# A two-layer hybrid block on one core: a block of matrix products ahead of the first projection, the first norm's factors in an earlier transfer, a new order of work in the mixers, and one gate half in another arithmetic

## The chip, the core and the metric

The kernel runs on 1 core of one Trainium2 chip. The metric is the device time of one execution in microseconds. Before the change the median of 3 runs is 876.97 us (876.23 to 877.3). The engines of the core work from queues of their own, each in the order in which its instructions were issued: the tensor engine (PE: weight loads and matrix products), the vector engine (DVE), the scalar engine (ACT), GpSimd (POOL), and SyncE (SP), which only issues transfers.

## The reference, cut to what matters

Two layers, 256 positions, width 1024. Each layer is a mixer and a feed-forward part, each behind an RMS norm.

```
def s5_mixer(u, ...):                       # u: 512 wide, 32 groups of 16
    bu = einsum('bsgh,gph->bsgp', uf, b)    # 64 complex states a group
    x = associative_scan(complex_affine_combine, (a, f * bu), axis=1)
    y = re(einsum('bsgp,ghp->bsgh', x, c)) + d * uf
    z_val, z_gate = split(gelu(y) @ w_glu, 2)
    return z_val * sigmoid(z_gate)

def hybrid_mixer(h, ...):
    u, q, k_cmp, v_cmp, k_sel, v_sel, k_win, v_win, nsa_gate, g_ssm, g_nsa = split(h @ w_in, ...)
    y_ssm = s5_mixer(u, ...) @ w_branch_ssm
    y_nsa = nsa_mixer(rope(q), rope(k_cmp), ...) @ w_branch_nsa   # 3 kinds of attention, 8 heads
    return (sigmoid(g_ssm) * y_ssm + sigmoid(g_nsa) * y_nsa) @ w_out

def conv_ffn(h, ...):
    a, b = split(h @ w_in, 2)               # 2 x 2816
    return (gelu(causal_conv3(a) + conv_b) * b) @ w_out

for l in range(2):
    x = x + hybrid_mixer(rmsnorm(x, norm_mix[l]), ...)
    x = x + conv_ffn(rmsnorm(x, norm_ffn[l]), ...)
return rmsnorm(x, norm_final)
```

## The kernel before, in words

Activations lie transposed: 128 features on the partitions, 8 blocks of features, 256 positions as the moving side of a product. Weights stream from HBM in blocks of 128x1024 (512 KB) through a ring of 5 buffers (`raw`, L142). SP issues these transfers in program order. The norm's per-feature factors (`g_mix`) are multiplied in before the products (`xg`, L424), its per-position factor afterwards, when a result is read from PSUM (`rb`, L403).

There are two arithmetics for a product of 128 features by 256 positions. In the first layer's mixer it is full precision (L413, L437): one product, which the trace holds as two records. Elsewhere (L164 to L166) both sides are split into a rounded high part and a remainder, and three products are summed: `wh*ah`, `wh*al`, `wl*ah`. There ACT makes the high part of each weight block (`wh`, L153), and DVE the remainder (`wl`, L155).

A mixer is written as a list of short items, `ORDER` (L55), one string for each layer. `A:q:h` are the input products of state-space group q (half h) and DVE's turn into rotated coordinates (`psb`, `bc`, `bs`, `z`), `B` and `C` the scans over the two position halves, `D` the products of states and rotation (`pr`) and the output products (`psy`). `kc`, `ks`, `q`, `v` are projections, `cw`, `ck`, `cv` the compressed keys and values, `ac`, `at` the attention over them, `as` the scores and softmax of the other two kinds, `av` their transposes and value products (`ps_t`, `pT`, `ps_o`). `g:m:i` is half i of gate m, 8 gates in all: 8 blocks of weights by 256 positions into one half of a PSUM bank (`ps_g`), and after the second half one multiplication on DVE and one tanh on ACT (`th`, L811, L814). The items are issued in this order; a scheduler then places each instruction on its engine by priority, and products marked `row()` stay together. The gates take turns with other projections in two PSUM banks (tag `mm`), all else has six (`aux`). Behind the items come the GLU (`ps_glu`), the branch products (`ps_br`) and the output projection.

At the start (L123 to L139, L941 to L945) SP issues the two halves of x and the first two weight blocks in turn, ACT the transfers of `ssp` (the state-space parameters) and `sp` (all other small parameters). ACT makes squares for the norm (L360, L363) and `xg`, and PE begins with `psu` (U, L437).

Of the kernel before, what the change touches and what calls it, by code (L numbers as in the profile page):

```python
# [4 lines left out]
F32 = mybir.dt.float32  # L5
F32R = mybir.dt.float32r
BF = mybir.dt.bfloat16
I32 = mybir.dt.int32
AF = mybir.ActivationFunctionType
# [4 lines left out]
L = 2  # L14
T = 256
KD = 8
NF = 22
NS = 16
# [21 lines left out]
for _name, _w in [("ropec", 256), ("ropes", 256), ("ident", 128), ("causal", 128),  # L40
# [8 lines left out]
ENG = dict(t0="VV", c0="V", t1="VV", c1="V", cy="G", nacc="V", ma="V", sw="VG", z="VV", pr="VVVVVVVV")  # L49

NRAW, NWH, NWL, NSS, NSW, NRT, NPT, NZ, NTH = 5, 3, 3, 4, 1, 2, 2, 2, 8
HP = (400, 0)
AHEAD = (3, 4, 5, 6)

ORDER = [o.split() for o in (  # L55
# [10 lines left out]


def chunk_plan():
# [19 lines left out]
def body(tc, ctx, d, out):  # L88
    from contextlib import ExitStack
    nc = tc.nc  # L90
    V, S, G, PE = nc.vector, nc.scalar, nc.gpsimd, nc.tensor
    pool = lambda name, bufs=1, **k: ctx.enter_context(tc.tile_pool(name=name, bufs=bufs, **k))
    cst = pool("cst")
    raws = pool("raws", NRAW)

    pad = lambda name, n: pool(name).tile([128, n // 4], F32, name=name)
    pad("pad0", 128)
    whs = pool("whs", NWH)
    pad("pad3", 128)
    wls = pool("wls", NWL)  # L100
# [1 line left out]
    pp = pool("pp")  # L102
# [3 lines left out]
    psm = pool("psm", 1, space=PSUM)  # L106
# [6 lines left out]
        o += n  # L113


    ssp = cst.tile([128, 3 * L * NS + 14], F32, name="ssp")
    cc = cst.tile([128, NCC], F32, name="cc")

    def cslice(name):
# [3 lines left out]
    x = pp.tile([128, KD, T], F32, name="x", tag="x")  # L123
    dram = pool("dram", 1, space=bass.MemoryType.DRAM)
    xd = dram.tile([128, KD, T], F32, name="xd")
    spt = [cst.tile([128, NSP], F32, name=f"sp{l}") for l in range(L)]
    S.dma_start(ssp, d["ssp"])
    S.dma_start(spt[0], d["sp"][0])
    nc.sync.dma_start(x[:, 0:4, :], d["xT"][:, 0:4, :])

    def sp(l, name):
        a, w = _cols[name]
        return spt[l][:, a:a + w]

    ones = cst.tile([128, 128], F32, name="ones")
    V.memset(ones, 1.0)
    zero2 = cst.tile([128, 2], F32, name="zero2")
    V.memset(zero2, 0.0)
    S.activation(zero2, zero2, AF.Square)  # L139


    def raw(l, nm):  # L142
        o, n = where[nm]
        t = raws.tile([128, CH], F32, name="raw", tag="raw")
        src = bass.AP(tensor=d["wst"].tensor, offset=128 * (l * per_layer + o), ap=[[n, 128], [1, n]])
        nc.sync.dma_start(t[:, :n], src)
        return t, n

    def split(l, nm):

        t, n = raw(l, nm)
        h = whs.tile([128, CH], F32R, name="wh", tag="wh")
        S.copy(h[:, :n], t[:, :n])  # L153
        lo = wls.tile([128, CH], F32R, name="wl", tag="wl")
        V.tensor_tensor(lo[:, :n], t[:, :n], h.bitcast(F32)[:, :n], op=OP.subtract)  # L155
        return h, lo
# [37 lines left out]
    par = cst.tile([128, 5, N2], F32, name="par")  # L194
# [154 lines left out]
    class Norm:  # L349
        def __init__(self, l, gname, x, split=True):  # L350
            self.x = x
            self.g = sp(l, gname)
            if split:
                self.ah = pp.tile([128, KD, T], F32R, name="ah", tag="ah")
                self.al = pp.tile([128, KD, T], F32R, name="al", tag="al")
            self.acc = wk.tile([128, T], F32, name="nacc", bufs=1)
# [47 lines left out]


    def mixer(l, nm, sc, first, mp, sm_):
        if l:
            ah, al = nm.ah, nm.al

        def proj(ps, w):  # L410
            if not isinstance(w, tuple):
                for k in range(KD):
                    PE.matmul(ps, w[:, k * 128:(k + 1) * 128], xg[:, k, :], start=k == 0, stop=k == KD - 1,  # L413
                              skip_group_check=True)
                return
            for k in range(KD):
                wh, wl = wt(w, k)
                mm3(ps, wh, wl, ah[:, k, :], al[:, k, :], k == 0, k == KD - 1)


        if l == 0:
            xg = mp.tile([128, KD, T], F32, name="xg", bufs=1)
            for k in range(KD):
                S.activation(xg[:, k, :], nm.x[:, k, :], AF.Copy, scale=nm.g[:, k:k + 1])  # L424
            for k in range(KD):
                nm.square(k)
# [3 lines left out]
        for h in range(2):  # L430
# [3 lines left out]
            for k in range(KD):  # L434
                for i in range(2):
                    if l == 0:
                        PE.matmul(psu[i][:, :T], cu[i][0][:, k * 128:(k + 1) * 128], xg[:, k, :], start=k == 0,  # L437
                                  stop=k == KD - 1, skip_group_check=True)
# [257 lines left out]
        at = {}  # L696
# [101 lines left out]

        th = {}

        def gates(m, h=None):

            if h != 1:
                th[m] = bank("ps_g")
            ps = th[m]
            for i in (0, 1) if h is None else (h,):
                n = f"g{8 * i + m}"
                proj(ps[:, i * T:(i + 1) * T], raw(l, n)[0] if l == 0 else split(l, n))
            if h == 0:
                return  # L810
            t = lt.tile([128, 2, T], F32, name="th", tag="th", bufs=NTH)  # L811
            tt(t, ps.rearrange("p (a t) -> p a t", a=2), rb[:, None, :].to_broadcast([128, 2, T]), OP.mult)
            S.activation(t, t, AF.Tanh, scale=0.5)
            th[m] = t  # L814

        def gates_held(m, h=None):

            with tc.issue_after(at["hold"].ins):
# [1 line left out]

        parts = {"kc": p_kc, "ks": p_ks, "q": p_q, "v": p_v, "cin": c_in, "cw": c_w1, "ck": c_k, "cv": c_v, "par": p_par,
                 "pf": p_pf, "tb": p_tb, "mb": p_mb, "mc": p_mc, "ac": a_cmp, "at": a_cmpt, "as": a_s, "av": a_v,
                 "g": gates, "gh": gates_held, "A": ssm_a, "B": ssm_b2, "C": ssm_c2, "D": ssm_d}
        for item in ORDER[l]:
            f, *a = item.split(":")
            parts[f](*map(int, a))
# [113 lines left out]

    nm = Norm(0, "g_mix", x, False)  # L941
    first = [raw(0, "u0")]
    nc.sync.dma_start(x[:, 4:8, :], d["xT"][:, 4:8, :])
    first += [raw(0, "u1"), None, None]
    nc.sync.dma_start(cc, d["cc"])  # L945
    identb = cst.tile([128, 128], BF, name="identb")
    V.tensor_copy(identb, cslice("ident"))
# [125 lines left out]
    return s  # L1073


def ssm_small(p):

    fact = [1.0]
    for i in range(1, 16):
        fact.append(fact[-1] * i)  # L1080
    sin = [1.0 / fact[13], -1.0 / fact[11], 1.0 / fact[9], -1.0 / fact[7], 1.0 / fact[5], -1.0 / fact[3], 1.0]
    cos = [-1.0 / fact[14], 1.0 / fact[12], -1.0 / fact[10], 1.0 / fact[8], -1.0 / fact[6], 1.0 / fact[4], -1.0 / fact[2]]
    c = np.array([sin, cos], np.float32).T.reshape(1, 14)
    return np.concatenate([np.concatenate(p, axis=2).reshape(128, -1), np.repeat(c, 128, axis=0)], axis=1)


def const_array():
# [50 lines left out]
```

## Time and profile before

| | |
|---|---|
| runs shown, median of 3 | 876.97 us |
| profiled execution | 873.18 us |
| its span, first to last instruction | 871.1 us |
| mean granted clock of the tensor engine | 0.963 |
| busy: PE, DVE, ACT | 93%, 79%, 48% |

The first mixer takes the time up to about 200 us, its output projection and the feed-forward part go to about 430, the second mixer to about 633, the rest to the end. In a row of the timeline the number before "us" is the start, the next the length, "x" the count of instructions merged, and the bracket the idle time ahead with what ended it. A product's record ends only when its result has drained, so records that follow each other overlap, and the pace is read from many of them.

### The profile page before, as it was taken

To read this page: it belongs to the slowest core of one execution; us is meant where nothing else is said; L and a number is where in the kernel's file an instruction comes from. 1 tells how busy PE (TensorE), PEld (TensorE's weight loads), DVE (VectorE), ACT (ScalarE), POOL (GpSimd) and SP (SyncE) were. 2 spreads that over 40 slices of the span, in tenths; PEclk is the share of its full clock that TensorE was granted. 3 is DMA by queue.
4 is the path that set the end of the run, shared out by engine and by line. 5 is a ranking of instruction groups with operands and counts; after the bars stand their busy time and mean duration, and the time that the engine had idled before them with its cause. 6 is when DMAs were issued, how large, how long until landed. Compare 5 with 4: busy or idle time off the path is not lost.

```text
span 871.1 us, 16396 instructions
## 1 busy us (share of the span) xinstructions
PE 808.7 (93%) x6456; PEld 733.6 (84%) x6456; DVE 689.6 (79%) x1325; ACT 421.6 (48%) x783; POOL 25.4 (3%) x58
## 2 busy tenths in 40 slices
PE   5998999899989999999998889986899999999994
PEld 5886787469989999999998579763699999999994
DVE  6999766957998988877857998858588888888553
ACT  3211136575544665556522247755546555555440
POOL 0001000000000000000001030100000000000000
PEclk9999999799999999999999899967999999999997
DMA  6647635205645666658744663411155565655631
GB/s 245 192 115 254 216 106 168 77 25 159 183 148 166 192 195 194 194 183 271 242 143 117 236 201 133 134 60 49 64 175 183 184 194 194 194 194 194 193 124 49
DMA packets 41773, 142.42 MB, mean 163 GB/s; under 512 B 5216, under 2 KB 6752, under 8 KB 41696
## 3 DMA queue, kind: packets, MB, share of 16 engines
q1 hardware_dynamic: 39712, 139.15, 50.2%
q10 hardware_dynamic: 1984, 2.23, 0.9%
q8 instruction: 50, 0.82, 0.4%
q14 instruction: 27, 0.22, 0.1%
HBM read 136.38 MB, written 2.10 MB: 159 GB/s over the span
## 4 chain that ended last, share of the span: by engine, by line
PE 76%; DVE 14%; DMA 3%; ACT 3%; issue 3%; POOL 0%; ACTq 0%; DVEq 0%; SPq 0%
PE ps_f L165 9%; PE ps_f L166 9%; PE ps_f L164 9%; PE ps_g L413 5%; PE ps_fo L166 5%; PE ps_fo L165 5%; PE ps_fo L164 5%; DVE z L575 3%; PE psu L437 2%; PE ps_g L165 2%; PE ps_br L164 2%; PE ps_g L166 2%; PE ps_br L165 2%; PE ps_br L166 2%; PE ps_g L164 2%
## 5 line engine op out<-in xcount | busy, mean ns | idle before, releaser
L153 ACT CAST wh<-raw 128x1024 fp32r<-128x1024 f32 (+1 forms) x199 | 207.4, 1046 | 219.8 <-PE ps_f L165 99.0
L155 DVE TENSOR_TENSOR wl<-raw,wh 128x1024 fp32r<-128x1024 f32 (+1 forms) x199 | 242.6, 1221 | 66.7 <-ACT wh L153 66.1
L165 PE MATMUL ps_f<-al,wh 128*128 128x256 f32 x704 | 195.4, 278 | 2.4 <-DVE al L208 2.4
L164 PE MATMUL ps_f<-ah,wh 128*128 128x256 f32 x704 | 195.4, 278 | 1.8 <-DVE x L208 1.2
L166 PE MATMUL ps_f<-ah,wl 128*128 128x256 f32 x704 | 195.2, 277 | 0.8 <-DVE wl L155 0.8
L165 PEld LDWEIGHTS ps_f<-al,wh 128*128 128x128 f32 x704 | 132.9, 189 | 2.6 <-DVE al L208 2.6
L164 PEld LDWEIGHTS ps_f<-ah,wh 128*128 128x128 f32 x704 | 132.9, 189 | 2.1 <-ACT wh L153 2.1
L166 PEld LDWEIGHTS ps_f<-ah,wl 128*128 128x128 f32 x704 | 133.0, 189 | 1.0 <-DVE wl L155 1.0
L165 PE MATMUL ps_fo<-fl,wh 128*128 128x256 f32 x352 | 97.0, 276 | 0.0
L164 PE MATMUL ps_fo<-fh,wh 128*128 128x256 f32 x352 | 96.9, 276 | 0.0
L166 PE MATMUL ps_fo<-fh,wl 128*128 128x256 f32 x352 | 96.8, 276 | 0.0
L164 PEld LDWEIGHTS ps_fo<-fh,wh 128*128 128x128 f32 x352 | 66.1, 188 | 0.0
L165 PEld LDWEIGHTS ps_fo<-fl,wh 128*128 128x128 f32 x352 | 66.1, 188 | 0.0
L166 PEld LDWEIGHTS ps_fo<-fh,wl 128*128 128x128 f32 x352 | 65.9, 188 | 0.1
L413 PE MATMUL ps_g<-xg,raw 128*128 128x256 f32 x256 | 59.8, 389 | 0.0
L413 PEld LDWEIGHTS ps_g<-xg,raw 128*128 128x128 f32 x256 | 48.6, 194 | 8.0 <-issue 1.2
L199 DVE TENSOR_TENSOR pr<-z,E 128x512 f32<-128x512 f32 x64 | 41.7, 700 | 6.8 <-PE psy L610 6.7
L208 DVE SCALAR_TENSOR_TENSOR cv<-ab,sp,cv 128x255 f32<-128x255 f32 (+1 forms) x88 | 41.8, 480 | 1.4
L575 DVE TENSOR_TENSOR_SCAN z<-rm,z 128x512 f32<-128x512 f32 x32 | 38.8, 1244 | 1.5 <-POOL z L199 1.5
L166 PE MATMUL ps_g<-ah,wl 128*128 128x256 f32 x128 | 37.2, 290 | 0.6 <-DVE wl L155 0.5
L165 PE MATMUL ps_g<-al,wh 128*128 128x256 f32 x128 | 37.2, 291 | 0.0
L164 PE MATMUL ps_g<-ah,wh 128*128 128x256 f32 x128 | 36.8, 288 | 0.0
(260 smaller groups left out, 1705.7 us busy)
## 6 DMA issues: line engine op xcount, KB each, us to landing
raw<-wst SPq DMA_DIRECT2D x248, 512.0 KB, 4.3
x<-xT SPq DMA_DIRECT2D x4, 512.0 KB, 5.0
raw<-wst SPq DMA_DIRECT2D x4, 420.0 KB, 3.8
xd<-x SPq DMA_DIRECT2D x2, 512.0 KB, 7.3
x<-xd SPq DMA_DIRECT2D x2, 512.0 KB, 4.4
sw<-rt SPq DMA_DIRECT2D x12, 64.0 KB, 3.1
sw<-rt ACTq DMA_DIRECT2D x12, 64.0 KB, 4.2
raw<-wst SPq DMA_DIRECT2D x2, 280.0 KB, 2.8
```

What stands on the lines that cost most here:

```text
L153: S.copy(h[:, :n], t[:, :n])
L155: V.tensor_tensor(lo[:, :n], t[:, :n], h.bitcast(F32)[:, :n], op=OP.subtract)
L164: PE.matmul(ps, wh, ah, start=start, stop=False, **k)
L165: PE.matmul(ps, wh, al, start=False, stop=False, **k)
L166: PE.matmul(ps, wl, ah, start=False, stop=stop, **k)
L199: return e.tensor_tensor(o, a, b, op=op)
L208: e.scalar_tensor_tensor(o, a, s, b, op0=op0, op1=op1)
L413: PE.matmul(ps, w[:, k * 128:(k + 1) * 128], xg[:, k, :], start=k == 0, stop=k == KD - 1, skip_group_check=True)
L437: PE.matmul(psu[i][:, :T], cu[i][0][:, k * 128:(k + 1) * 128], xg[:, k, :], start=k == 0, stop=k == KD - 1, skip_group_check=True)
L575: V.tensor_tensor_scan(f, rt.rearrange("p a t -> p (a t)"), f, 0.0, op0=OP.mult, op1=OP.add)
```

## The change

There are five edits. Ahead of U, PE multiplies a 128x128 block of ones by itself 14 times, into a PSUM tile that nothing reads. The first norm's 8 factor columns are appended to `ssp`, and `xg` takes them from there. The second half of x is issued after the second weight block instead of before it. An item `sa` in the first mixer splits `xg` into high part and remainder, and an item `gs` makes a gate half in the arithmetic of the three products; it is used for `g:1:1` alone. Both strings of `ORDER` are new.

```
 NRAW, NWH, NWL, NSS, NSW, NRT, NPT, NZ, NTH = 5, 3, 3, 4, 1, 2, 2, 2, 8
+WARM = 14
 ORDER = [
-    ('par tb:0 pf q:1 q:0 mb kc cin tb:1 A:0:0 A:0:1 ks B:0 v A:1:0 A:1:1 g:0:0 g:0:1 g:1:0 g:1:1 cw:0:0 cw:0:1 '
+    ('par tb:0 q:1 kc mb q:0 pf cin tb:1 A:0:0 A:0:1 B:0 ks v A:1:0 A:1:1 sa g:0:0 g:0:1 g:1:0 cw:0:0 cw:0:1 '
...
-     'as:1:1:1:1 B:3 av:1:0 D:2:0 D:2:1 g:5:0 g:5:1 g:7:0 g:7:1 g:0:0 g:0:1 C:3 g:3:0 g:3:1 g:6:0 g:6:1 av:1:1 '
+     'as:1:1:1:1 D:2:0 g:5:0 g:5:1 g:7:0 g:7:1 g:0:0 g:0:1 D:2:1 g:3:0 g:3:1 C:3 g:2:1 g:6:0 g:6:1 av:1:1 D:3:0 '
...
-    pad("pad0", 128)
+    pad("pad0", 96)
...
-    ssp = cst.tile([128, 3 * L * NS + 14], F32, name="ssp")
+    ssp = cst.tile([128, 3 * L * NS + 22], F32, name="ssp")
...
+    nc.sync.dma_start(x[:, 0:4, :], d["xT"][:, 0:4, :])
     S.dma_start(ssp, d["ssp"])
     S.dma_start(spt[0], d["sp"][0])
-    nc.sync.dma_start(x[:, 0:4, :], d["xT"][:, 0:4, :])
...
+    warm = psm.tile([128, 512], F32, name="warm", tag="aux", bufs=6)
+    for i in range(WARM):
+        PE.matmul(warm[:, :128], ones, ones, start=i == 0, stop=i == WARM - 1, skip_group_check=True)
...
-            self.g = sp(l, gname)
+            self.g = ssp[:, 3 * L * NS + 14:] if l == 0 and gname == "g_mix" else sp(l, gname)
...
-        def gates(m, h=None):
+        def p_sa():
+
+            nonlocal ah, al, xg
...
+            ah = pp.tile([128, KD, T], F32R, name="ah", tag="ah")
+            al = pp.tile([128, KD, T], F32R, name="al", tag="al")
+            for k in range(0, KD, 4):
+                split_act(ah[:, k:k + 4, :], al[:, k:k + 4, :], xg[:, k:k + 4, :])
+
+        def gates_other(m, h=None):
+            gates(m, h, l == 0)
+
+        def gates(m, h=None, sp=l > 0):
...
-                proj(ps[:, i * T:(i + 1) * T], raw(l, n)[0] if l == 0 else split(l, n))
+                proj(ps[:, i * T:(i + 1) * T], split(l, n) if sp else raw(l, n)[0])
...
     first = [raw(0, "u0")]
+    first += [raw(0, "u1"), None, None]
     nc.sync.dma_start(x[:, 4:8, :], d["xT"][:, 4:8, :])
-    first += [raw(0, "u1"), None, None]
```

On PE the program now starts with the ones, and a projection of q stands between the two halves of U. Before:

```order
L437 MATMUL psu<-xg,raw 128x256 x16
L382 MATMUL ps_n<-ones,nacc 128x1 x2
L382 MATMUL ps_n<-ones,sq 128x1 x2
L437 MATMUL psu<-xg,raw 128x256 x16
L413 MATMUL ps_q_405<-xg,raw 128x256 x10
```

and now:

```order
L144 MATMUL warm<-ones 128x128 x14
L442 MATMUL psu<-xg,raw 128x256 x16
L417 MATMUL ps_q_404<-xg,raw 128x256 x8
L387 MATMUL ps_n<-ones,nacc 128x1 x2
L442 MATMUL psu<-xg,raw 128x256
L387 MATMUL ps_n<-ones,sq 128x1 x2
```

The sums of the norm (`ps_n`) move behind that half of q.

On ACT at the start the block xg is now made in two parts, with the casts of `sa` (`ah`) between the squares. Before:

```order
L360 ACTIVATE nacc<-x 128x256
L363 ACTIVATE sq<-x 128x256 x3
L424 ACTIVATE xg<-x,sp_101 128x256 x8
L363 ACTIVATE sq<-x 128x256 x4
L159 CAST Bh<-raw 128x1024
```

and now:

```order
L365 ACTIVATE nacc<-x 128x256
L368 ACTIVATE sq<-x 128x256
L429 ACTIVATE xg<-x,ssp 128x256 x4
L368 ACTIVATE sq<-x 128x256
L164 CAST ah<-xg 128x1024
L368 ACTIVATE sq<-x 128x256
L429 ACTIVATE xg<-x,ssp 128x256 x4
```

The first half of xg stands behind one square instead of three, the second half behind a cast.

On DVE near the end of the second mixer, from the last group's turn into rotated coordinates (`bc` to `z`) on; `mx` are row maxima of the scores, `su` belongs to the softmax. Before:

```order
L199 TENSOR_TENSOR bs<-psb,E 128x512
L754 TENSOR_REDUCE mx_6549<-ps_s 128x2
L754 TENSOR_REDUCE mx_6554<-ps_s 128x2
L199 TENSOR_TENSOR z<-bc,bs 128x2x2x128 x2
L203 TENSOR_SCALAR mx_6549<-mx_6549 128x2
L203 TENSOR_SCALAR mx_6554<-mx_6554 128x2
L575 SCALAR_TENSOR_TENSOR z<-rm,z 128x512 x2
L754 TENSOR_REDUCE mx_6572<-ps_s 128x2
L754 TENSOR_REDUCE mx_6577<-ps_s 128x2
L203 TENSOR_SCALAR mx_6572<-mx_6572 128x2
L575 SCALAR_TENSOR_TENSOR z<-rm,z 128x512 x2
```

and now:

```order
L204 TENSOR_TENSOR bs<-psb,E 128x512
L204 TENSOR_TENSOR z<-bc,bs 128x2x2x128 x2
L580 SCALAR_TENSOR_TENSOR z<-rm,z 128x512 x2
L759 TENSOR_REDUCE mx_6555<-ps_s 128x2
L759 TENSOR_REDUCE mx_6560<-ps_s 128x2
L208 TENSOR_SCALAR mx_6555<-mx_6555 128x2
L580 SCALAR_TENSOR_TENSOR z<-rm,z 128x512 x2
L208 TENSOR_SCALAR mx_6560<-mx_6560 128x2
L160 TENSOR_TENSOR wl<-raw,wh 128x1024
L204 TENSOR_TENSOR th<-ps_g,rb 128x512
L160 TENSOR_TENSOR wl<-raw,wh 128x1024
```

The maxima now follow the first scan, and weight subtractions (`wl`) and multiplications (`th`) of gates, of which there were none behind this place, come after it.

## Rows read from the trace of the kernel before

**Rows 1.** The page's line of busy time, share of the span, instructions.
```profile
PE 808.7 (93%) x6456; PEld 733.6 (84%) x6456; DVE 689.6 (79%) x1325; ACT 421.6 (48%) x783; POOL 25.4 (3%) x58
```
**Rows 2.** The page's 40 slices: granted clock in tenths.
```profile
PEclk9999999799999999999999899967999999999997
```
**Rows 3.** Stretches: length; busy us of PE, PEld, DVE, ACT, POOL; clock; DMA; GB/s.
```profile
27.00:60.00 33.00, 33.00 (x173) 28.32 (x171) 31.85 (x76) 6.16 (x12) 0.00 (x0) 1.00 0.60 175
165.00:175.00 10.00, 8.43 (x43) 2.92 (x41) 10.00 (x22) 6.63 (x24) 0.78 (x4) 0.50 0.32 106
300.00:400.00 100.00, 100.00 (x885) 100.00 (x884) 83.66 (x126) 59.37 (x94) 0.00 (x0) 1.00 0.64 196
500.00:523.00 23.00, 20.01 (x158) 17.81 (x157) 22.62 (x30) 9.65 (x13) 7.10 (x8) 0.93 0.64 207
523.00:560.00 37.00, 37.00 (x320) 32.73 (x319) 31.77 (x60) 28.20 (x65) 3.30 (x6) 1.00 0.40 133
574.00:592.00 18.00, 18.00 (x93) 11.95 (x92) 10.79 (x29) 9.53 (x30) 0.00 (x0) 0.53 0.00 1
592.00:602.00 10.00, 4.46 (x24) 3.13 (x22) 9.96 (x17) 3.43 (x14) 0.77 (x4) 0.66 0.32 105
602.00:620.00 18.00, 14.38 (x128) 7.19 (x127) 11.35 (x24) 11.79 (x28) 0.00 (x0) 1.00 0.01 1
```
**Rows 4.** Timeline of PE at the start: start, length, what.
```profile
8.77 10.11 PE L437 MATMUL psu<-xg,raw 128*128 128x256 f32 x32 [8.77 <-ACT xg L424]
...
19.53 7.15 PE L437 MATMUL psu<-xg,raw 128*128 128x256 f32 x32
```
**Rows 5.** The products of tile psu: ns shortest/median/longest, first and last start.
```profile
L437 PE MATMUL psu<-xg,raw x64: 379/379/792, 8.8 to 26.3; 128*128 128x256 f32 x64
```
**Rows 6.** Timeline of DVE and ACT at the start.
```profile
0.83 0.17 DVE L136 MEMSET ones<- 128x128 f32 x1 [0.83 <-PEq L1130]
...
5.79 0.42 ACT L360 ACTIVATE nacc<-x 128x256 f32<-128x256 f32 x1 [2.62 <-DMA x<-xT]
...
8.23 3.28 ACT L424 ACTIVATE xg<-x,sp 128x256 f32<-128x256 f32 x8
```
**Rows 7.** Timeline of SP, then DMA issues of 2 to 3 us with landing.
```profile
1.64 0.43 SPq L943 DMA_DIRECT2D x<-xT  x1
2.12 0.95 SPq L146 DMA_DIRECT2D raw<-wst  x1
...
x<-xT SPq DMA_DIRECT2D x1, 512.0 KB, 7.3
raw<-wst SPq DMA_DIRECT2D x1, 512.0 KB, 8.1
```
**Rows 8.** Timelines of ACT and DVE: the split of B.
```profile
31.74 1.05 ACT L159 CAST Bh<-raw 128x1024 fp32r<-128x1024 f32 x1 [16.93 <-DMA raw<-wst]
...
33.72 1.22 DVE L160 TENSOR_TENSOR Bl<-raw,Bh 128x1024 fp32r<-128x1024 f32 x1
```
**Rows 9.** Timelines of PE and DVE in the middle of the first mixer.
```profile
84.66 0.41 PE L667 MATMUL ps_h<-cc,hs 128*128 128x32 f32 x2 [2.98 <-ACT hs L663]
...
83.02 0.67 DVE L199 TENSOR_TENSOR th<-ps_g,rb 128x512 f32<-128x512 f32 x1
```
**Rows 10.** Timeline of PE near the end of the first mixer.
```profile
164.39 1.19 PE L746 MATMUL ps_s<-ksw,q 64*128 64x512 f32 x5 [2.61 <-ACT pt L758]
```
**Rows 11.** The second mixer's end: timelines of DVE and PE, tiles wl and th.
```profile
587.22 0.69 DVE L199 TENSOR_TENSOR bc<-psb,E 128x512 f32<-128x512 f32 x1
...
598.65 1.12 PE L782 MATMUL ps_o<-pT,vt 128*64 128x256 f32 x4 [5.45 <-ACT pT L779]
...
619.41 0.51 PE L164 MATMUL ps_glu<-y,wh 128*128 128x256 f32 x2 [1.41 <-ACT y L159]
...
L155 DVE TENSOR_TENSOR wl<-raw,wh x33: 716/1216/1761, 453.8 to 639.3; 128x1024 fp32r<-128x1024 f32 x30, 128x840 fp32r<-128x840 f32 x2, 128x560 fp32r<-128x560 f32 x1
...
L199 DVE TENSOR_TENSOR th<-ps_g,rb x8: 636/680/692, 516.0 to 569.0; 128x512 f32<-128x512 f32 x8
```

More of the change, by code (lines that the diff above doesn't have):

```diff
@@ L406, in mixer @@
     def mixer(l, nm, sc, first, mp, sm_):
-        if l:
-            ah, al = nm.ah, nm.al
+        ah, al = (nm.ah, nm.al) if l else (None, None)
         def proj(ps, w):
@@ L418, in proj @@
                 mm3(ps, wh, wl, ah[:, k, :], al[:, k, :], k == 0, k == KD - 1)
+        xg = None
         if l == 0:
@@ L799, in mixer @@
         th = {}
-        def gates(m, h=None):
+        def p_sa():
+            nonlocal ah, al, xg
+            if l:
+                xg = mp.tile([128, KD, T], F32, name="xg", bufs=1)
+                for k in range(KD):
+                    S.activation(xg[:, k, :], nm.x[:, k, :], AF.Copy, scale=nm.g[:, k:k + 1])
+                return
+            ah = pp.tile([128, KD, T], F32R, name="ah", tag="ah")
[5 more added lines that the diff above has]
+        def gates(m, h=None, sp=l > 0):
             if h != 1:
@@ L822, in mixer @@
                  "pf": p_pf, "tb": p_tb, "mb": p_mb, "mc": p_mc, "ac": a_cmp, "at": a_cmpt, "as": a_s, "av": a_v,
-                 "g": gates, "gh": gates_held, "A": ssm_a, "B": ssm_b2, "C": ssm_c2, "D": ssm_d}
+                 "g": gates, "gh": gates_held,
+                 "gs": gates_other, "sa": p_sa, "A": ssm_a, "B": ssm_b2, "C": ssm_c2, "D": ssm_d}
         for item in ORDER[l]:
@@ L1073, in pack_small, with ssm_small @@
     return s
-def ssm_small(p):
+def ssm_small(p, g):
     fact = [1.0]
@@ L1083, in ssm_small @@
     c = np.array([sin, cos], np.float32).T.reshape(1, 14)
-    return np.concatenate([np.concatenate(p, axis=2).reshape(128, -1), np.repeat(c, 128, axis=0)], axis=1)
+    return np.concatenate([np.concatenate(p, axis=2).reshape(128, -1), np.repeat(c, 128, axis=0), g], axis=1)
 def const_array():
@@ L1126 @@
                                          np.repeat(a["ssm_log_dt"][l], 64).reshape(16, 128).T], axis=1)
-                               for l in range(L)]),
+                               for l in range(L)], a["norm_mix"][0].reshape(8, 128).T),
         "wst": np.concatenate([pack_layer(a, l) for l in range(L)]),
```

16 rows, old and new, of the table ORDER are left out of this document.

## The prediction, made blind

> **What bounds the kernel now.** I read the page's line of busy times first: the tensor engine (PE) is busy 93% of the span, the vector engine (DVE) 79%, the scalar engine (ACT) 48% [rows 1]. Taken alone this says that only less PE work can help. The slices say otherwise: the row of granted clock dips to 6 and 7 in the slices behind 566 us [rows 2]. So next I read the table by stages [rows 3]. In the feed-forward part PE runs 885 products in 100 us at full clock; that is 113 ns for one product of 256 columns in the three-product form, and nothing waits. The two mixers are different. From 500 to 523 us, in the second mixer, PE is busy 20.0 of 23 us and DVE 22.6: DVE bounds there. From 523 to 560 PE is busy all 37 us and DVE 31.8: both are close to their limit. From 574 to 592 PE counts as busy, but at a granted clock of 0.53, and from 592 to 602 it has 4.5 us of work in 10. The first mixer has a similar patch: 8.4 of 10 us at clock 0.50 from 165 to 175. The change touches these mixers and the start, not the feed-forward part, so the stages outside count as unchanged.
>
> **The start.** PE begins at 8.77 us; its first 32 product records take 10.11 us and the next 32, of the same form, 7.15 us [rows 4]. The longest of them takes 792 ns against a median of 379 [rows 5], a factor of two, so it ran at the lower of the two clock levels, 1.2 GHz, though the row of the first stretch prints no dip. Ahead of the slow ones the engine did nothing at all; ahead of the fast ones it made products. The 14 products of ones are 28 records of 128 columns. At half of 7.15/32 us each they take 3.1 us at the upper level and twice that, 6.3 us, at the lower. The fill that they need is DVE's first instruction, from 0.83 us [rows 6], so they end between 4 and 7.5 us. They cost U nothing, since its second weight block lands later than that, as follows.
>
> U needs xg, and that stands behind three squares and the large block of small parameters: ACT starts xg at 8.23 us, though x has landed by 5.79 [rows 6]. With the factors in the first, small block, xg follows one square, at about 6.5 us. Then the second weight block decides: it was issued at 2.1 us as the fourth transfer and took 8.1 us to land, thus 10.2; as the third it takes the place of the half of x that was issued at 1.6 us and landed 7.3 later, at 8.9 [rows 7]. From 8.9 us, 32 records in 7.15 us end at 16.0, against 18.9 before: 2.9 us.
>
> What keeps this from counting in full is DVE, which is busy 31.85 of 33 us from 27 to 60 [rows 3]. The new part "sa" gives it two subtractions of 1024 columns, each 1.22 us as for Bl, and ACT two casts of 1.05 us [rows 8]. DVE falls back by 2.4 us, less what of its 1.15 us of idle in that stretch they fill. I take 2 us of the 2.9 as kept; the ends are 0 and 2.9.
>
> **The middle of the first mixer.** At 81.7 us PE runs dry: the two products ps_h wait 2.98 us for the copy hs on ACT, which stands behind a tanh that waits for a DVE multiplication at 83.02 [rows 9]. Now one gate half is put off, and only one tanh stands ahead of hs. PE is there earlier by 8 full-precision products, 16 records at 7.15/32 = 0.22 us, 3.6 us. But the load of ACT's function table behind hs remains, and PE has less to do meanwhile. I take 0, with ends of -2 and +2. The gate half itself: 3.6 us of records become 24 products at 113 ns, 2.7 us; DVE pays 1.22 more and ACT 1.05, beside PE. I take 0, with ends of -0.9 and +1.2.
>
> **The end of the first mixer.** PE waits 2.61 us there [rows 10], and the 8.4 us at half clock [rows 3] cost 4.2: some 7 us could come back. The input products of the last state-space group now stand ahead of the scores of the second query half, so their scans no longer meet the row maxima on DVE. One gate of 16 full-precision products, 7 us, stands among the last scores. The chain softmax, transpose, product stays. I take -2.5, with ends of 0 and -7.
>
> **The second mixer.** This is the largest term. Before, all 384 gate products stand ahead of the last group's input products, which DVE reads at 587.2 us; the dense GLU stream comes at 619.4 [rows 11]. In the new order I count 106 of the 384 behind them. Ahead, PE loses 106 x 113 ns = 12.0 us; DVE loses five weight subtractions (1.216 us each) and two multiplications (0.68 us), 7.4 us [rows 11]. Of the stretch from 523 to 587 the first 37 us are PE's by a narrow margin, so the gain lies between 7.4 and 12; I take 9, since DVE soon binds.
>
> Behind, PE had 5.45 us of one wait and half a clock [rows 3, 11], so 12 us of products fit. DVE gets two subtractions and three multiplications, 4.5 us, and two GLU subtractions earlier, 2.4 us, less four products of state and rotation done before, 2.4 us. It had 10.0 of 10 and 11.4 of 18 us from 592 to 620, so 21.3 becomes about 26 of 28. A queue that full does not serve the softmax at once: I lengthen the tail by 3 us, between 0 and 6. The term is -6, with ends of -12 and +1. The wait added is the longer hold of a PSUM bank, below. In front of it, up to the casts of the selected keys, DVE has the same seven gate subtractions in both orders; I take nothing there, -2 to +2.
>
> **Sum.** -2 + 0 + 0 - 2.5 - 6 = -10.5 us. The profiled execution took 873.18 us, of which 871.1 are span; it becomes 862.7. The runs have a median of 876.97, 3.8 above it; so the median becomes 866.5 us.
>
> **A rule against it.** The order shows that the gate whose second half is put off holds one of the two PSUM banks that the gates use, from its first half until near the end; five gates in between share the other, and each must wait for DVE's multiplication of the one before. DVE starts such a multiplication after what is queued: four products of 0.69 us and one subtraction of 1.216 are 4.0 us [rows 11]. Behind PE's waiting product, which is the next gate's first, stand the scores and input products of the same block, so all of these wait too. The Trainium skill, "TensorE: Matmul & The Clock Gate", section "A second HAM failure mode: psum-queue depth-cycling", says that small idle times between groups that cycle through PSUM banks can bring the clock down again and again. The trace of before agrees only in part: with both banks in use the stretch of 523 to 560 us shows clock 1.00. By that rule the mechanism would come out as the slow rival below, with its price from rows.
>
> **The rivals.** *Moved, not won* (0.20): DVE bounds the second mixer from end to end, so what leaves the stretch ahead comes back in the tail, and the sum keeps the first mixer: 876.97 - 4.5 = 872.5. For it speaks 22.6 of 23 us on DVE [rows 3]; against it, DVE is busy only 11.4 of 18 us from 602 to 620 [rows 3]. The same time comes out if the ones do not lift the clock and the second mixer wins half.
>
> *One bank* (0.10), the slower side: five gates have four gaps of 4.0 us; attention products cover half, so 8 us are left. If the clock then falls for as long as from 574 to 592, another 18 us at half speed cost 9. Against -10.5 this gives +6.5: 883.5. With some 60% of both it is +0, so it decides from about 1.2 us of idle in each gap with the clock down. For it: five gates, one bank. Against: three of the gaps are filled with scores, transposes or input products of the next group.
>
> *Both ends won* (0.15): the tail hides everything (-12), and the first mixer's end gives 5: 876.97 - 2 - 5 - 12 = 858.
>
> *Forecast* (0.55): 861.5 to 871.5 as its own range, 866.5 as the point.
>
> **How the numbers follow.** A measurement of this kernel can tell about 0.2% from no change, 1.75 us. Faster than 875.2: all of the forecast, all of both ends won, most of moved (0.14) and a little of the bank (0.01): 0.55 + 0.15 + 0.14 + 0.01 = 0.85. Within: 0.05 of moved and 0.02 of the bank, 0.07. Slower: 0.07 of the bank and 0.01 of moved, 0.08. The range from 858 to 875.5 leaves out the bank's slow part and the farther half of both ends won.
>
> **What would show it.** Right: the first U product at about 7.5 to 9 us with 32 records in some 7.2 us; the wait at ps_h no longer than 5 us; the last input products of the second mixer read near 575 us less the first mixer's gain; no stretch of clock 0.5 of 17 us behind them; DVE busy above 0.85 from there to the GLU stream, which starts near 609. Wrong: idle PE ahead of a gate's first product with DVE's multiplication as releaser (one bank); a tail longer than 40 us from last input products to GLU (moved); U's records still at 0.32 us each (the ones do not help). If the start is won but the first mixer still ends at the same time, DVE took it.

## The result, and the profile after

The changed kernel takes 863.64 us (median of 4 runs, 861.6 to 866.28) against 876.6 us for the kernel before beside it (4 runs, 875.92 to 877.3). The ratio is 0.9854 with an interval of 0.9826 to 0.9882: 12.8 us less, between 10.3 and 15.3. The prediction said 866.5 us, 10.5 less. The two profiled executions lie closer together, 863.77 and 873.18 us: the execution whose rows stand above was about 3 us below the median of its kernel, so the stages below account for 9.4 us.

The sum came out near, and its terms did not. A landmark is the first or last record of one tile on PE; its lead is its start before minus its start after.

| landmark on PE | before | after | lead, us |
|---|---|---|---|
| first mixer: first psb | 47.78 | 43.93 | 3.85 |
| first ps_br | 199.97 | 192.18 | 7.79 |
| feed-forward: first ps_f | 247.71 | 239.91 | 7.80 |
| first ps_fo | 375.10 | 363.80 | 11.30 |
| second mixer: first psu | 432.66 | 423.29 | 9.37 |
| last psb | 587.58 | 571.57 | 16.01 |
| first ps_br | 630.23 | 620.94 | 9.29 |
| last feed-forward: first ps_fo | 797.31 | 788.16 | 9.15 |

The start gave 3.9 us and the rest of the first mixer as much again. The second mixer gains 6.6 us up to its last input products and has given all of it back by its end. The page's line of busy times after, for [rows 1], and its slices of granted clock, for [rows 2]:

```profile
PE 816.8 (95%) x6492; PEld 741.9 (86%) x6492; DVE 691.4 (80%) x1328; ACT 420.9 (49%) x784; POOL 30.7 (4%) x58
...
PEclk9998989999999999999998998859999999999997
```

PE is busy for 8.1 us more in a span that is 9.1 shorter; 5.1 of the 8.1 are the ones. The 6 and 7 behind 566 us have become a 5 at 560: the slow patch has moved forward, it has not gone. The 7 behind 152 us is gone too, but 8s stand behind 65 and 108 us, where there were none. The timeline of PE at the start, for [rows 4]:

```profile
1.05 5.09 PE L144 MATMUL warm<-ones 128*128 128x128 f32 x28 [1.05 <-DVE E L304]
7.26 7.15 PE L442 MATMUL psu<-xg,raw 128*128 128x256 f32 x32 [1.12 <-DMA raw<-wst]
14.77 3.72 PE L417 MATMUL ps_q<-xg,raw 128*128 128x256 f32 x16 [0.36 <-DMA raw<-wst]
```

Ahead of U stand the ones; then the first 32 records of U take 7.15 us, as only the later ones did before, not 10.11. What U waits for at 7.26 is its weight block, no longer xg. The stretches of the table of stages, for [rows 3] (columns as there):

```profile
27.00:60.00 33.00, 33.00 (x173) 28.02 (x172) 32.86 (x81) 6.80 (x14) 0.00 (x0) 1.00 0.60 177
165.00:175.00 10.00, 10.00 (x82) 5.50 (x82) 9.11 (x19) 9.05 (x24) 0.00 (x0) 1.00 0.34 120
300.00:400.00 100.00, 100.00 (x885) 100.00 (x884) 80.14 (x117) 57.17 (x87) 0.00 (x0) 1.00 0.65 199
557.00:579.00 22.00, 22.00 (x97) 15.23 (x98) 17.34 (x39) 10.50 (x31) 0.78 (x4) 0.53 0.03 11
579.00:608.00 29.00, 28.70 (x249) 21.16 (x247) 20.80 (x36) 19.60 (x46) 0.00 (x0) 1.00 0.41 128
```

The end of the first mixer (165 to 175) has PE full at clock 1.00, where it had 8.4 of 10 us at 0.50. In the second mixer the stretch at 0.53 is still there, 22 us long where the one shown before had 18. The tail behind it has PE busy 28.7 of 29 us and DVE 20.8: it is PE that is full there, not DVE. In the middle of the first mixer the wait for hs is 2.40 us, as against 2.98 [rows 9]; at the second GLU stream it is 2.06 us for y [rows 11]:

```profile
76.42 0.63 PE L672 MATMUL ps_h<-cc,hs 128*128 128x32 f32 x2 [2.40 <-ACT hs L668]
...
610.38 0.50 PE L169 MATMUL ps_glu<-y,wh 128*128 128x256 f32 x2 [2.06 <-ACT y L164]
```

The three waits of PE near the end of the first mixer, 2.61 [rows 10], 1.57 and 0.94 us, have no successor: from 130 to 192 us nothing on PE waits in the profile after.

### The profile page after: what moved, and what is told of

Its sections match the earlier page's. It is cut to its first block, busy times and chain, and to the rows that moved or that the text cites. A ratio compares the mean times of both kernels' runs of the same rounds, so it can differ in the third digit from the quotient of the medians.

```text
span 862.0 us, 16474 instructions
## 1 busy us (share of the span) xinstructions
PE 816.8 (95%) x6492; PEld 741.9 (86%) x6492; DVE 691.4 (80%) x1328; ACT 420.9 (49%) x784; POOL 30.7 (4%) x58
## 4 chain that ended last, share of the span: by engine, by line
PE 74%; DVE 11%; DMA 6%; ACT 4%; issue 4%; POOL 0%; SPq 0%; DVEq 0%; ACTq 0%
PE ps_f L170 9%; PE ps_f L169 9%; PE ps_f L171 9%; PE ps_g L417 5%; DMA raw<-wst 4%; PE ps_fo L171 3%; PE ps_fo L170 3%; PE ps_fo L169 3%; PE ps_s L751 2%; PE psy L615 2%; PE ps_o L787 2%; PE ps_br L169 2%; PE ps_br L170 2%; PE ps_br L171 2%; PE ps_g L169 2%
## 5 line engine op out<-in xcount | busy, mean ns | idle before, releaser
L417 PEld LDWEIGHTS ps_g<-xg,raw 128*128 128x128 f32 x240 | 45.6, 198 | 9.0 <-issue 2.1
L204 DVE TENSOR_TENSOR pr<-z,E 128x512 f32<-128x512 f32 x64 | 42.0, 704 | 10.5 <-PE psy L615 10.4
L169 PE MATMUL ps_g<-ah,wh 128*128 128x256 f32 x136 | 43.2, 318 | 1.5 <-DVE th L204 0.8
L171 PE MATMUL ps_g<-ah,wl 128*128 128x256 f32 x136 | 41.8, 309 | 2.4 <-DVE wl L160 2.4
L170 PE MATMUL ps_g<-al,wh 128*128 128x256 f32 x136 | 42.1, 310 | 0.0
```

Of the source, the lines that this page charges most:

```text
L169: PE.matmul(ps, wh, ah, start=start, stop=False, **k)
L170: PE.matmul(ps, wh, al, start=False, stop=False, **k)
L171: PE.matmul(ps, wl, ah, start=False, stop=stop, **k)
L204: return e.tensor_tensor(o, a, b, op=op)
```

## The experiments

Each was timed in five rounds beside the kernel before, whose median was 876.31 us with the first four, 874.87 with the next four, 875.47 with the last four. The differences to it below are the ratios times 875.5 us.

### The parts, placed by the scheduler

**The start alone.** Both strings of `ORDER` are the old ones:

```
 ORDER = [o.split() for o in (
-    ('par tb:0 q:1 kc mb q:0 pf cin tb:1 A:0:0 A:0:1 B:0 ks v A:1:0 A:1:1 sa g:0:0 g:0:1 g:1:0 cw:0:0 cw:0:1 '
+    ('par tb:0 pf q:1 q:0 mb kc cin tb:1 A:0:0 A:0:1 ks B:0 v A:1:0 A:1:1 g:0:0 g:0:1 g:1:0 g:1:1 cw:0:0 cw:0:1 '
...
```

> The changed kernel with both old sequences of items: only the ones, the factors in the first block and the transfer of x are new. The two traces put the first psb of the first mixer 3.85 us earlier after the change (47.78 to 43.93) and the first ps_br 7.8 us earlier. Theory: the start's 3.9 us are kept to the end of the mixer, since PE is busy there throughout and DVE's queue has room for all of them; 876.6 - 3.9 = 872.7 us, between 871.5 and 874.5, and the first ps_br near 196.1. Rival (my prediction): DVE keeps about half, 874.6 us. Second rival: DVE, busy 31.85 of 33 us from 27 to 60, takes all of it, 876.6 us within 0.7, and the first ps_br stays at 200.0.

871.43 us, ratio 0.9947 (0.9931 to 0.9962): 4.6 less. The time lies at the edge of the theory's range (871.5), its place does not fit at all: the first ps_br stands at 205.7, not 196.1. The first mixer ended 5.7 us later than before, and the second one, whose string is the old one too, took 191.6 us from first psu to first ps_br instead of 197.6. The order of the instructions shows what else had changed: times shifted by a few microseconds ahead, and the scheduler placed the instructions behind differently. On PE, DVE and ACT the second mixer stands in another order though its string is the same.

**No ones.** `WARM = 14` becomes `WARM = 0`.

> The changed kernel without its 14 products of ones, nothing else. Theory: the first 32 records of U take 10.1 us again instead of 7.15, the first psb comes 3 us later, and these 3 us stay to the end: 863.6 + 3 = 866.6 us, between 865.3 and 868. Rival: the ones matter only for the clock row of the first microseconds and the second block of U is late anyway, so the first psb moves by less than 1 us: 863.6 to 864.6 us.

865.27 us, ratio 0.9877 (0.9862 to 0.9892): 1.6 above the changed kernel by the medians, but with intervals that overlap, and just between theory and rival. The first psb comes 1.0 us later (44.94), not 3. The question comes back below, with the mixers held.

**The old second string**, all else as changed.

> The changed kernel with the old sequence of the second mixer, all else new. In the traces the second mixer starts with a lead of 9.4 us (first psu of the layer, 432.7 and 423.3), has a lead of 16.0 at the last psb, and leaves with 9.1 at its last ps_br. Theory: the new sequence of the second mixer is worth nothing, 863.6 us within 1.8. Rival (my prediction): it is worth 6 us, 869.6 us, between 867.5 and 872.

866.07 us, ratio 0.9882 (0.9867 to 0.9897). By the medians 2.4 above the changed kernel, between theory and rival.

**The old first string**, so without `sa` and `gs`, all else as changed.

> The changed kernel with the old sequence of the first mixer (so without the split of xg and the split gate half), all else new. Theory: the sequence of the first mixer and the split half are worth the 3.9 us by which the lead grows from the first psb (3.85) to the first ps_br (7.8), 867.5 us, between 866.3 and 869, with ps_br at 196. Rival (my prediction): 2.5 us, 866.1 us. Second rival: the old sequence keeps the first feed-forward part's half clock of 3.4 us (253.7 to 257.1 before, none after) and its two waits for weights (1.3 us and a slow patch), 3.5 us in all, so that the time is 871 us.

883.9 us, ratio 1.0084 (1.0068 to 1.01): 7.4 slower than before. None of the three numbers holds. This kernel differs from the first of these runs by the second string alone, and is 12 us slower; in the changed kernel that string had seemed to win 2.4. A term that changes its sign like this is not the string's own.

### The parts, held in place

So the places were taken out of the hands of the scheduler. A list `PLACE` says for each instruction of a mixer where it stood in another kernel, and each is chained behind the one that stood ahead of it on its engine, without a wait:

```
+    def place(traced, span):
+        last = {}
+        for i in np.cumsum(np.frombuffer(zlib.decompress(base64.b85decode(PLACE)), np.int16))[slice(*span)]:
+            ins = traced[int(i)]
+            if ins.engine in last:
+                tc.add_manual_dep(ins, last[ins.engine].name, mybir.DependencyInfo(
+                    mybir.DependencyClass.NoSync, mybir.DependencyReason.DATA), reason="place")
+            last[ins.engine] = ins
...
             nm = mixer(l, nm, sc, first, *[es.enter_context(tc.tile_pool(name=f"{n}{l}", bufs=2)) for n in ("mix", "mis")])
+        place(nc.cur_bb.bb.instructions[n0:], ((0, 0), (0, None))[l])
```

**The second mixer alone**: the kernel before with the new second string and this list, from the changed kernel.

> The kernel before, with the second mixer as it stands in the changed kernel, instruction for instruction on every engine (a list of positions holds the scheduler to it); all ahead of the second mixer is as before. This isolates the new sequence of the second mixer. The old sequence alone in the changed kernel gave 866.07 us against 863.64, but with the old first mixer the new second one gave 883.9 against 871.4, and the scheduler had placed the same items differently each time. Theory: with its placement the second mixer of the changed kernel is worth 0 to 3 us, 873.5 to 876.5 us. Rival (my prediction): 6 us, 870.4 us. Second rival: it is bad behind the old first mixer whatever its placement, about 12 us worse, 888 us.

875.93 us, ratio 1.0017 (1.0001 to 1.0033): 1.5 slower. The time lies in the theory's range, but beside its own kernel before it is no gain of 0 to 3 us: the second mixer won nothing.

**Old first, new second, held**: the run at 883.9 us with the same list.

> The run with the old first mixer and the new second one (883.9 us), with the second mixer held to the placement that it has in the changed kernel; ahead of it nothing differs from that run. Theory: the 883.9 us came from the scheduler's placement of the second mixer alone, which changes when times ahead of it shift; held, the time falls to that of the start alone, 871.4 us less 0 to 3, so 868 to 872 us. Rival: the old first mixer leaves the second one something else (buffers, transfers, the clock) that makes the new sequence slow, and the time stays at 884 us within 2.

879.36 us, ratio 1.0052 (1.0034 to 1.007). Both fail: holding the second mixer took 4.5 us off, and what is left above the kernel before lies ahead of it. The first ps_br stands at 206.4 here and at 204.8 and 205.7 in the two other runs with the new start and the old first string; before it was 200.0.

**The second mixer of before in the changed kernel**: old second string, places from the kernel before.

> The changed kernel with the second mixer as it stands in the kernel before, instruction for instruction on every engine. Against the changed kernel this prices the second mixer without the scheduler's own shifts. Theory: the second mixer is worth 0 to 3 us, 863.6 to 866.6 us. Rival (my prediction): 6 us, 869.6 us.

863.28 us, ratio 0.9877 (0.9854 to 0.9901); the changed kernel has 863.64 and 0.9854. The theory holds: by the medians the whole gain is there without the new second mixer, by the ratios 10.8 us of 12.8, with intervals that overlap.

**The new second string alone**, placed by the scheduler: the kernel before with one string changed.

> The kernel before with the new sequence of the second mixer, placed by the scheduler as it comes. Theory: its time differs from that of the same sequence held to the placement of the changed kernel by more than 2 us, with no sign that I can name beforehand; anything from 872 to 888 us. Rival: the placement matters little, and the two agree within 1.5 us.

889.07 us, ratio 1.0157 (1.0132 to 1.0181): 13.7 slower, against 1.5 for the same string held. The theory holds, by more than its range. On PE, DVE and ACT the two programs order the second mixer differently. The stretches of the second mixer up to its last psb and from there to its first ps_br, then the end of the first mixer, show where; first the run held:

```profile
431.33:578.09 146.76, 130.19 (x1030) 110.48 (x1029) 118.65 (x215) 61.99 (x137) 16.81 (x24) 0.91 0.43 140
578.09:628.06 49.97, 45.08 (x363) 35.63 (x359) 35.30 (x60) 30.18 (x70) 0.78 (x4) 0.97 0.30 96
160.00:190.00 30.00, 24.88 (x168) 12.91 (x167) 22.02 (x51) 21.95 (x65) 0.78 (x4) 0.83 0.12 36
```

and then the one placed by the scheduler:

```profile
435.69:587.60 151.91, 136.81 (x1073) 115.78 (x1072) 121.03 (x216) 65.55 (x136) 17.70 (x24) 0.90 0.44 139
587.60:646.27 58.67, 44.44 (x319) 31.43 (x315) 33.06 (x60) 30.08 (x72) 1.82 (x4) 0.85 0.22 72
160.00:190.00 30.00, 25.14 (x150) 11.69 (x147) 24.70 (x54) 19.23 (x59) 0.77 (x4) 0.72 0.11 36
```

The tail is 8.7 us longer with fewer records in it, at 0.85 of the clock instead of 0.97, and the stretch ahead 5.2 longer. What PE waited for in that tail and, last, in the whole second mixer (wait, us in total, times, longest):

```profile
PE ps_t L777 <- ACT pb L768: 4.7, 2, 3.4
PE ps_o L782 <- ACT pT L779: 3.9, 2, 2.1
PE ps_t L777 <- ACT pt L768: 2.3, 2, 1.7
...
PE ps_g L164 <- DVE th L199: 3.9, 4, 1.8
```

The softmax chain waits again, and the last row is the rival called one bank: four waits of a gate's first product for the multiplication before it. The rows from 160 to 190 are a matter of their own: up to the second mixer both programs are the same, instruction for instruction, and yet the clock there was 0.83 in one profiled execution and 0.72 in the other, and the first ps_br stood at 198.8 and 204.5. Most of these 5.7 us arose earlier: at the last input products of the first mixer the two were already 3.8 us apart (153.10 and 156.91). The same stretch of 45 us ahead of that, first in the run held, then in the other:

```profile
80.00:125.00 45.00, 41.29 (x295) 32.59 (x287) 33.64 (x63) 8.93 (x18) 2.21 (x8) 0.96 0.59 193
80.00:125.00 45.00, 40.71 (x259) 31.95 (x251) 33.26 (x59) 9.11 (x18) 2.41 (x9) 0.89 0.57 186
```

### The terms one by one

**The start, held**: the run of the start alone, with both mixers in their places of the kernel before.

> The kernel before with the start's edits alone (ones, factors in the first block, transfer of x), and both mixers held, instruction for instruction on every engine, to their places in the kernel before. In the run with both old sequences left to the scheduler the first psb came 2.4 us earlier, and yet the first mixer ended 5.7 us later, in another placement. Theory: held, the 2.4 us are kept and nothing else changes, 2.4 us below the kernel before, within 1.2. Rival (my prediction's term): 2 us; it cannot be told from the theory. Second rival: DVE takes them, no change within 0.8. Third rival: the start itself, not the placement, brings the slow end of the first mixer, 5 us above the kernel before.

870.06 us, ratio 0.9944 (0.9922 to 0.9967): 4.9 less, between 2.9 and 6.8. The third rival fell: the first ps_br stands at 198.5. That the late end of the first mixer with the new start (204.8 to 206.4 in three executions) belongs to the scheduler's placement is likely but not shown, since the old places gave 204.5 in one execution too. One part of the start is missing here: in the held places ACT makes xg behind three squares, as before, so U begins at 8.45 us and not at 7.26.

**The first mixer, held**: the new first string with `sa` and `gs` in its places of the changed kernel, the second mixer as before, and the old start.

> The kernel before with the first mixer's new sequence alone, the split gate half with it, held to the places that it has in the changed kernel; the second mixer is held to its places in the kernel before, and the start is the old one (no ones, factors in the large block, x ahead of the second weight block). Theory: the first mixer is worth what the whole change gives less the start, 11.6 - 2.4 = 9.2 us below the kernel before, within 2. Rival (my prediction's terms for the middle, the half and the end of the first mixer): 2.5 us below. Second rival: start and first mixer need each other, 5 to 6 us below.

865.56 us, ratio 0.9893 (0.9865 to 0.9921): 9.4 less, between 6.9 and 11.8. The theory holds. This is the largest term. (The new places of xg on ACT are in it, though the factors come late: U begins at 8.19 us.) Its end of the first mixer, as in the row from 160 to 190 above (0.83 and 0.72 there):

```profile
160.00:190.00 30.00, 30.00 (x224) 19.07 (x223) 17.37 (x43) 22.72 (x64) 0.00 (x0) 1.00 0.28 85
```

**No ones, held**: the changed kernel with `WARM = 0` and both mixers in their own places.

> The changed kernel without the ones, both mixers held to their places in the changed kernel. Without holding them the ones were worth 1.6 us (865.27 against 863.64). Theory: 32 records at half clock cost 3.0 us and the mixer loses that much at its first psb and to the end, 866.6 us. Rival: the wait of U's second block and of what follows takes part of it, 1 to 2 us, 864.6 to 865.6 us.

866.82 us, ratio 0.9894 (0.9867 to 0.9921): 3.2 above the changed kernel by the medians, of the size that the theory gives, though the intervals overlap. The start of U shows the mechanism, first here and then in the run without ones above:

```profile
7.22 9.89 PE L474 MATMUL psu<-xg,raw 128*128 128x256 f32 x32 [7.22 <-DMA raw<-wst]
7.40 8.64 PE L441 MATMUL psu<-xg,raw 128*128 128x256 f32 x32 [7.40 <-DMA raw<-wst]
```

9.89 and 8.64 us for the 32 records, against 7.15 from the same start of 7.2 to 7.4 us: the ones save 1.5 to 2.7 us there. In the held run 2.1 us of it are left at the first psb (46.01 against 43.93) and 1.4 at the first ps_br (193.58 against 192.18). That the ones are worth 3 us of the kernel's time is not shown.

**A better version**: the changed kernel with the old second string, in the places that the scheduler gave it in the run of the start alone.

> The changed kernel with the old sequence of the second mixer, held to the places that the scheduler gave it in the run with the start alone, where the stretch from the layer's first psu to its first ps_br took 191.6 us against 197.6 in the kernel before and 197.7 in the changed one. Theory: these places carry the 6 us with them, 863.6 - 6 = 857.6 us, within 2, faster than both kernels. Rival: the 191.6 us came from how the clock fell in that one profiled execution, and the time is 863 us within 1.5.

859.12 us, ratio 0.9812 (0.9782 to 0.9843): 16.5 less than before, and 4.5 below the changed kernel by the medians (its runs went from 856.85 to 862.62, those of the changed kernel from 861.6 to 866.28; the intervals of the two ratios still overlap a little). The theory holds within its 2 us: the places carried their time along. The whole second mixer there, first in the run of the start alone:

```profile
436.34:627.98 191.64, 170.89 (x1386) 141.44 (x1384) 153.51 (x275) 93.18 (x205) 18.38 (x28) 0.91 0.41 132
```

and then in this kernel:

```profile
424.62:616.24 191.62, 173.53 (x1386) 142.34 (x1384) 154.38 (x275) 93.38 (x205) 20.30 (x28) 0.91 0.41 132
```

Read over all profiles, first psu to first ps_br: the places of the kernel before took 197.6, 195.5, 197.7 and 195.3 us (in it, and held in three others); those of the changed kernel 197.7, 197.2, 196.7, 196.7 and 196.3; the scheduler's other results 191.6 and 198.2 for the old string, 204.4 and 210.6 for the new one. The places decide, far more than the string. The two short ones of the first four, 195.5 and 195.3, are those behind the new first mixer; why is open.

## Why the sum was right and its terms were not

That the sum came out is luck: the terms of the start and of the end of the first mixer were too small, that of the second mixer too large, and the errors cancelled.

**The start** was put at -2, up to -2.9; held, it measures -4.9 (-6.8 to -2.9). The ones did as forecast: they took 5.09 us and ended at 6.14, and U ran with full-speed records. Two steps failed. The first is "then the second weight block decides". That block, issued at 1.64 us, took this long to land, about as forecast:

```profile
raw<-wst SPq DMA_DIRECT2D x1, 512.0 KB, 6.9
```

So it came at 8.5 us, but U had begun at 7.26 with the first block and did not pause. Its first 32 records ended at 14.41, 4.5 us earlier than before, where 16.0 and 2.9 had been forecast. The rows of before hint at it: there too U began (8.77) ahead of the second block (10.2). The second step is the reserve for DVE. DVE is full from 27 to 60 us (32.86 of 33), and most of the lead stays: 3.85 us at the first psb, and at the first ps_c 7.65 less the put-off gate half of 3.6 us. The two subtractions of `sa` are in this row of the tile al on DVE:

```profile
L165 DVE TENSOR_TENSOR al<-xg,ah x2: 1220/1223/1226, 9.0 to 13.1; 128x1024 fp32r<-128x1024 f32 x2
```

They stand at 9.0 and 13.1 us, ahead of the full stretch; DVE was busy 19.6 of the first 27 us before and is 21.1 now. So they cost at most the 0.6 us between 4.5 and 3.85.

**The middle of the first mixer and the split half** were put at 0. The wait for hs went from 2.98 to 2.40 us, but the sum had no term for the clock there. Two stretches of 30 us and the whole mixer (first psb to first ps_br), before:

```profile
70.00:100.00 30.00, 25.83 (x174) 19.41 (x172) 24.81 (x40) 4.80 (x9) 2.29 (x8) 0.94 0.66 220
100.00:130.00 30.00, 30.00 (x204) 25.55 (x203) 22.16 (x53) 7.98 (x27) 1.49 (x6) 1.00 0.48 150
47.78:199.97 152.19, 142.89 (x952) 106.22 (x951) 118.44 (x230) 61.03 (x167) 5.65 (x22) 0.96 0.43 137
```

and after:

```profile
65.00:95.00 30.00, 26.64 (x186) 19.36 (x188) 29.17 (x46) 4.18 (x8) 6.66 (x9) 0.89 0.69 237
95.00:125.00 30.00, 30.00 (x200) 24.56 (x196) 24.82 (x59) 13.22 (x39) 1.49 (x6) 0.89 0.36 113
43.93:192.18 148.25, 144.89 (x959) 108.53 (x958) 122.14 (x237) 62.30 (x169) 10.60 (x22) 0.95 0.45 141
```

By the clock alone (0.11 of 60 us against 0.06 of 30) the two stretches lost some 5 us more than before, an estimate. Over the whole mixer the mean clock is 0.95 against 0.96: what came back at its end went in its middle. What is won in the profile is idle time of PE, 3.4 us against 9.3.

**The end of the first mixer** was put at -2.5, up to -7. With the middle it measures -9.4 (-6.9 to -11.8) by the medians and -4.4 in the profiles (first psb to first ps_br, 152.2 before and 147.75 held with the old start). The mechanism was right for this stretch: scores and scans no longer wait for each other, PE's waits are gone, and the clock is 1.00 from 125 us on. The size was wrong, in part since one profile priced a mixer whose clock differs from execution to execution: the same old instructions ended 5.7 us apart at ps_br, and the profile that I read is near the better of the two. How often each occurs was not measured. The profiled executions of the kernel before and of the run with the first mixer held, 873.18 and 865.4 us, are 7.8 us apart: 4.9 of that stands at the first ps_br, and 2.3 arose in the second mixer, whose places are the same in both (197.6 and 195.3 us). So the gap between -4.4 and -9.4 stays open in part.

**The second mixer** was put at -6; it measures +1.5 (0.1 to 2.9) alone, and between 0 (by the medians) and -2 (by the ratios) when it is taken out of the changed kernel. Ahead, -9 was forecast and -6.6 came; behind, +3 was forecast and +6.7 came. These are the stretches from the first psu to the last psb and on to the first ps_br, before:

```profile
432.66:587.58 154.92, 140.86 (x1146) 120.96 (x1145) 123.70 (x220) 73.17 (x150) 16.48 (x24) 0.91 0.47 150
587.58:630.23 42.65, 32.47 (x244) 21.58 (x242) 30.98 (x56) 23.20 (x59) 0.77 (x4) 0.87 0.15 50
```

and after:

```profile
423.29:571.57 148.28, 132.08 (x1030) 111.40 (x1029) 119.44 (x217) 62.62 (x140) 16.84 (x24) 0.88 0.43 139
571.57:620.94 49.37, 45.97 (x359) 35.74 (x357) 35.11 (x58) 29.80 (x66) 0.78 (x4) 0.93 0.30 97
571.57:610.38 38.81, 36.45 (x280) 26.66 (x278) 29.27 (x50) 25.11 (x58) 0.78 (x4) 0.92 0.31 96
```

116 records left the first stretch for the second: 106 of gates, as counted, and 10 of the GLU. The step that failed is "12 us of products fit" behind the last input products. They fit into 10.2 us of idle time only in part: PE's busy time grew by 13.5 us, its idle time shrank by 6.8, and the tail grew by the rest. Of the half clock that I had counted on as room, the stretch from 574 to 592 us lies for the larger part ahead of the last psb; after the change 557 to 579 us is as slow, and in the tail the clock rose only from 0.87 to 0.93. PE had 1386 records over the mixer in both kernels, and 173.3 us of busy time before against 178.0 after. So the rival "moved, not won" (0.20) was right about this mixer, for another reason: it said that DVE would bind, and PE did. From the last input products to the GLU stream (571.57 to 610.38, the last row) PE is busy 36.5 of 38.8 us and DVE 29.3, 0.75 where I had asked for more than 0.85. Its time of 872.5 was wrong, as the first mixer and the start made up for it.

**One bank** fell for the changed kernel: one wait of 0.83 us for `th` on PE (at 506.75) is all there is. In another placement of the same string it showed, with 3.9 us in four waits, about half of its price of 8. The Trainium skill, "TensorE: Matmul & The Clock Gate", section "A second HAM failure mode: psum-queue depth-cycling", would make such small gaps bring the clock down. No run here isolates that: the placement with the four waits also waits 10.9 us for the softmax in its tail, and the clock falls to 0.53 after the change without them.

**Both terms together.** Start and first mixer, measured apart, sum to -14.3, give or take 3.1 (from their two intervals); the changed kernel with the second mixer of before shows -10.8 (-8.7 to -12.8). Whether they overlap or only scatter stays open, and neither held run has both the early factors and the early xg. With the second mixer's +1.5 the three sum to -12.8, which is what was measured, but at give or take 3.4 that proves little. The feed-forward part that the prediction called unchanged took 127.4 us from first ps_f to first ps_fo before and 123.9 after; in the other runs it lies between 123.9 and 127.4 with no edit in it, so I count it as scatter. It was one third of the lead in the profiles at that place, and 1.9 us of it were gone at the second mixer.

## What to carry to other kernels

Where a scheduler places the instructions, a run with one part undone is not the change less that part: hold the places first, then compare. The room in a tail is its idle time, and not all of it fills: here 6.8 of 10.2 us did. Half-clock time is no room until the clock has been seen to come back, and a clock that recovers in one stretch is a gain only when it is read over the whole stage. A term read from one profile of a stretch whose clock differs between executions needs a second profile before it is priced.

## What the runs showed that was not expected

The same instructions of the first mixer ran at different clocks in different executions: from 160 to 190 us it was 0.83 in two and 0.72 in another, from 80 to 125 us 0.96 and 0.89, and the first ps_br stood at 198.8, 200.0 and 204.5 us. The clock also fell where PE did not idle at all: from 95 to 125 us after the change PE is busy 30.00 of 30 us at 0.89. A placement of one mixer carried its time into another kernel almost exactly (191.64 and 191.62 us). And the 73 items of the second mixer, in the order of the same string, took between 196.3 and 210.6 us, by the places of their instructions.
